# Order edges on VectorE kept in the gate-up groups of a hybrid encoder layer and dropped in its down and output projections

## The chip, the core and the metric

The kernel runs on one core of one Trainium2 chip. The metric is the device time of one execution, in microseconds. The core's engines that matter here are TensorE (PE in the profile), VectorE (DVE), ScalarE (ACT), GpSimd (POOL) and SyncE (SP), which issues nearly all transfers from memory.

## The reference

One encoder layer on 256 tokens of width 2048, all in float32: a gated feed-forward block, a mixer of two head groups, a second gated feed-forward block, each between two RMS norms.

```python
def swiglu(x, w_gate_up, w_down):
    gate, up = jnp.split(x @ w_gate_up, 2, axis=-1)          # 2048 -> 2 x 5632
    return (jax.nn.silu(gate) * up) @ w_down                 # 5632 -> 2048
...
    ff = swiglu(rms_norm(x, pre_norm_ffn1[layer]), w_ffn1_gate_up[layer], w_ffn1_down[layer])
    x = x + 0.5 * rms_norm(ff, post_norm_ffn1[layer])
    h = rms_norm(x, pre_norm_mix[layer])
    q_h, i_h, f_fwd, f_bwd, g_h, q_a, k_a, v_a = jnp.split(h @ w_mix_in[layer], split_at, axis=-1)
    y_h = hgrn2_mixer(...)          # gated linear recurrence, both directions, 8 heads
    y_a = window_attention(...)     # 8 heads, +-128 tokens
    mixed = jnp.concatenate([y_h, y_a], axis=-1) @ w_mix_out[layer]
    x = x + rms_norm(mixed, post_norm_mix[layer])
    ff = swiglu(rms_norm(x, pre_norm_ffn2[layer]), w_ffn2_gate_up[layer], w_ffn2_down[layer])
    x = x + 0.5 * rms_norm(ff, post_norm_ffn2[layer])
```

## The kernel before, in words

**Split operands.** Every float32 weight tile is written as a sum of two parts of a shorter format: a high part `h`, which ScalarE makes with a copy (line 191), and a lower part `l = raw - h`, which VectorE makes with a subtraction (line 192). A product of two split operands is three matmuls (line 447, method `three`): high by high, high by lower, lower by high. `split_half` (lines 180 to 188) splits one half, 128x1024, of a raw weight tile of 128x2048. Raw tiles lie in a ring of three, with a fourth one from the first gate-up group on and in the output projection (`rooms` in the feed-forward blocks); the `h` and the `l` tiles lie in two pools of five buffers each. A raw tile is loaded in two transfers of 512 KB, one for each half, and a transfer starts when the last reader of the old contents of that half is done.

**Units.** A stage of weights is worked off in units of 256 input rows by 1024 output columns. A plain unit (`plain`) takes 8 products, that is 24 matmuls. A mixed unit (`seven`) uses seven products instead of eight, a Strassen form with sums of blocks on both sides, and takes 21 matmuls. Its right-hand side costs VectorE three additions over the raw tile, in place: first `four` (line 480, 128x1024, two block sums at once), then the block `b22` (line 483, 128x512), then `b21` (line 484, 128x512, "the last addition"). Line numbers:

| step of `seven` | engine and line | what it needs |
|---|---|---|
| first block: `h`/`l`, or `ha`/`la` in the down stages and the output projection | ACT 191, DVE 192 | first half of the raw tile |
| `lower`: parts of the second half | ACT 191, DVE 192 | second half of the raw tile |
| three additions | DVE 480, 483, 484 | 480: first block split; 483: `lower` split and 480; 484: 483 |
| `upper`: parts of the summed first half | ACT 191, DVE 192 | 480 |
| `third`: parts of the summed second half | ACT 191, DVE 192 | 484 |

TensorE takes the seven products in the order first block, `lower`, `lower`, `upper`, `upper`, `third`, `third`.

**Stages.** The gate-up stages (class `Gated`, flag `AHEAD = False`) have 11 groups of 8 units, three of them mixed (two in group 1). The down stages and the output projection (class `Pairs`, flag `AHEAD = True`) have two runs each, one for each half of the output columns: 22 units a run in a down stage, 11 of them mixed; 8 units a run in the output projection, 2 of them mixed. In these, where a mixed unit is followed by a plain one, the plain unit's raw tile is loaded early and its first half (below: `v0`) is split between `upper` and `third` of the mixed unit (`begin_next`, lines 532 to 537); its second half (`v1`) comes after `third`. The input projection of the mixer, between them, has no mixed units but uses the same `split_half`.

**What sets the order.** The order of instructions in an engine's queue is not that of the program. A planner goes through the program when it is built; whenever an engine is free by its reckoning, it appends the earliest instruction of the program that is ready by its reckoning, so that a later instruction that is ready passes an earlier one that isn't yet. On the chip each queue is then worked off strictly in that order. `tc.issue_after(ins)` adds order edges: what its block puts on the engine of `ins` is queued behind `ins`. There is no wait in it, only a place in the queue. Here `last["sums"]` holds the newest `b21` addition, a VectorE instruction, so lines 184 to 187 tie the subtraction of line 192, and not ScalarE's copy, behind the last addition of the mixed unit that is newest in the program:

```python
        with ExitStack() as queued:
            if "sums" in last:
                queued.enter_context(tc.issue_after(last["sums"].ins))
            split_act(h, l, part)
```

The subtraction of the first block (`la`) is not made by `split_half` and has no such edge; nor have the additions.

Of the kernel before, what the change touches and what calls it, by code (L numbers as in the profile page):

```python
# [17 lines left out]
ALU = mybir.AluOpType  # L18
# [19 lines left out]
def hymba_layer_kernel(  # L38
# [25 lines left out]
    nc = tc.nc  # L64
# [15 lines left out]
    def pa():  # L80
        return psum.tile([P, 512], F32, tag="pa", name=nm("pa"))

    def pb():
        return psum.tile([P, 512], F32, tag="pb", name=nm("pb"))
# [64 lines left out]
    def load(src, between=None):  # L149
        raw = new_raw()  # L150
        if len(src.shape) == 4:

            dst = raw.rearrange("p (a n b) -> p a n b", a=src.shape[1], n=src.shape[2])
            parts = [(dst[:, a], src[:, a]) for a in range(src.shape[1])]
        else:
            n = src.shape[1]
            dst = raw.rearrange("p (a b) -> p a b", a=n)
            parts = [(dst, src)]
            if n == 2:
                parts = [(dst[:, a], src[:, a]) for a in range(2)]  # L160
        for i, (to, of) in enumerate(parts):
            if i and between:
                between()
            nc.sync.dma_start(to, of)
        return raw
# [14 lines left out]
    def split_half(raw, i, hp=hip, lp=lop):  # L180
        part = raw[:, i * 1024 : (i + 1) * 1024]
        h = hp.tile([P, 1024], F32R, tag="h", name=nm("h"))
        l = lp.tile([P, 1024], F32R, tag="l", name=nm("l"))
# [4 lines that stand above are left out]
        return h, l  # L188

    def split_act(hi, lo, src):  # L190
        nc.scalar.copy(hi, src)  # L191
        nc.vector.tensor_tensor(lo, src, hi.bitcast(F32), ALU.subtract)  # L192
# [37 lines left out]
    last = {}  # L230
# [179 lines left out]
    class Blocks:  # L410
# [58 lines left out]
        def seven(self, u, aside=None):  # L469

            self.left_early(u)
            raw = load(self.source(u))
            if aside:
                aside()
            b11, b12, b21, b22 = (raw[:, i * 512 : (i + 1) * 512] for i in range(4))
            four = raw.rearrange("p (i c) -> p i c", i=4)
            h, l = self.one_block()
            split_act(h, l, b11)
            lower = split_half(raw, 1)
            nc.vector.tensor_tensor(  # L480
                four[:, 0:2], four[:, 0::3], four[:, 1:2].to_broadcast([P, 2, 512]), ALU.add
            )
            nc.vector.tensor_tensor(b22, b11, b22, ALU.add)  # L483
            last["sums"] = nc.vector.tensor_tensor(b21, b22, b21, ALU.add)  # L484
            upper = split_half(raw, 0)
            if aside:
                aside()
            third = split_half(raw, 1)
            if not self.p:
                self.p = [pa(), pa(), pb(), pb()]  # L490
            a, w = self.tiles[u], self.left_sums(u)

            def lhs(k, m):
                return [a[:, k, i, m * P : (m + 1) * P] for i in range(2)]

            def summed(j):
                return [w[:, j, i, :] for i in range(2)]

            def rhs(two, n):
                return [x[:, n * 512 : (n + 1) * 512] for x in two]  # L500

            for at, left, right in (
                (("p", 0), lhs(0, 0), (h, l)),
                (("c", 0, 0), lhs(1, 0), rhs(lower, 0)),
                (("c", 0, 1), summed(S4), rhs(lower, 1)),
                (("p", 1), summed(S1), rhs(upper, 0)),
                (("p", 3), summed(S3), rhs(upper, 1)),
                (("p", 2), summed(S2), rhs(third, 1)),
                (("c", 1, 0), lhs(1, 1), rhs(third, 0)),
            ):  # L510
                self.three(at, *left, *right)
# [1095 lines left out]
```

## Time and profile before

| | |
|---|---|
| median of three runs | 1856.46 us (1854.08 to 1858.31) |
| the profiled execution | 1852.33 us, with a span of 1850.5 us |
| granted TensorE clock, mean | 0.999 |
| TensorE busy | 1828.6 us (99%) |
| VectorE busy | 1647.2 us (89%) |
| ScalarE busy | 1109.1 us (60%) |

The span is the time from the first to the last instruction that was profiled. "Idle before" is the time that an engine stood idle just before an instruction, and the releaser is what ended it. On SyncE all instructions are those of a queue that issues transfers; its time is waiting.

### The profile page before, as it was taken

To read this page: it belongs to the slowest core of one execution; us is meant where nothing else is said; L and a number is where in the kernel's file an instruction comes from. 1 tells how busy PE (TensorE), PEld (TensorE's weight loads), DVE (VectorE), ACT (ScalarE), POOL (GpSimd) and SP (SyncE) were. 2 spreads that over 40 slices of the span, in tenths; PEclk is the share of its full clock that TensorE was granted. 3 is DMA by queue.
4 is the path that set the end of the run, shared out by engine and by line. 5 is a ranking of instruction groups with operands and counts; after the bars stand their busy time and mean duration, and the time that the engine had idled before them with its cause. 6 is when DMAs were issued, how large, how long until landed. Compare 5 with 4: busy or idle time off the path is not lost.

```text
span 1850.5 us, 23957 instructions
## 1 busy us (share of the span) xinstructions
PE 1828.6 (99%) x8604; PEld 1517.0 (82%) x8604; DVE 1647.2 (89%) x2076; ACT 1109.1 (60%) x1470; POOL 33.3 (2%) x61
## 2 busy tenths in 40 slices
PE   9999999999999999999999999999999999999997
PEld 7888888888878777888888888888888888878776
DVE  7999999999999998577787798899999999989997
ACT  6555566565555556577677566555655555555553
POOL 1000000000000000000000000000000000000000
PEclk9999999999999999999999999999999999999999
DMA  8666566666877675655554565666666656778774
GB/s 286 200 229 210 194 203 218 211 201 215 283 256 266 228 248 197 217 177 174 168 181 153 187 218 184 202 231 214 208 221 222 212 195 199 254 260 269 244 254 169
DMA packets 192056, 400.45 MB, mean 216 GB/s; under 512 B 11976, under 2 KB 59168, under 8 KB 191168
## 3 DMA queue, kind: packets, MB, share of 16 engines
q1 hardware_dynamic: 188416, 387.24, 63.5%
q0 software_dynamic: 3520, 11.67, 1.6%
q8 instruction: 67, 1.10, 0.2%
q14 instruction: 53, 0.43, 0.1%
HBM read 383.12 MB, written 15.75 MB: 216 GB/s over the span
## 4 chain that ended last, share of the span: by engine, by line
PE 49%; issue 29%; DVE 12%; DMA 6%; ACT 3%; POOL 0%; SPq 0%; DVEq 0%; ACTq 0%; POOLq 0%
PE pa L447 16%; PE pb L447 15%; PE pa L322 8%; DVE l L192 7%; PE pa L327 4%; ACT h L191 2%; DMA raw<-in_w_ffn_down_dram 1%; DMA rooms<-in_w_ffn_down_dram 1%; DVE raw L480 1%; DMA raw<-in_w_ffn_gate_up_dram 1%; PE pa L377 1%; PE pa L376 1%; PE pa L375 1%; DVE raw L483 1%; DMA raw<-in_w_mix_out_dram 1%
## 5 line engine op out<-in xcount | busy, mean ns | idle before, releaser
L191 ACT CAST h<-raw 128x1024 fp32r<-128x1024 f32 (+1 forms) x691 | 682.4, 1014 | 425.0 <-DVE raw L484 118.9
L192 DVE TENSOR_TENSOR l<-raw,h 128x1024 fp32r<-128x1024 f32 (+1 forms) x691 | 795.2, 1174 | 77.9 <-ACT h L191 37.4
L447 PE MATMUL pa<-h,xt 128*128 128x512 f32 x1176 | 405.7, 391 | 0.0
L447 PE MATMUL pb<-h,xt 128*128 128x512 f32 x1060 | 368.9, 390 | 0.0
L447 PEld LDWEIGHTS pa<-h,xt 128*128 128x128 f32 x1176 | 220.8, 188 | 44.8
L447 PEld LDWEIGHTS pb<-h,xt 128*128 128x128 f32 x1060 | 198.9, 188 | 41.7 <-DVE xt L247 0.5
L447 PE MATMUL pa<-l,xt 128*128 128x512 f32 x588 | 229.5, 390 | 0.5 <-DVE l L192 0.5
L447 PE MATMUL pb<-l,xt 128*128 128x512 f32 x530 | 206.4, 389 | 0.0
L191 ACT CAST h<-rooms 128x1024 fp32r<-128x1024 f32 x138 | 142.1, 1050 | 90.1 <-DVE rooms L484 43.4
L192 DVE TENSOR_TENSOR l<-rooms,h 128x1024 fp32r<-128x1024 f32 x138 | 166.8, 1221 | 26.8 <-ACT h L191 26.3
L322 PE MATMUL pa<-xt,h 128*128 128x512 f32 x672 | 164.7, 394 | 0.0
L447 PE MATMUL pb<-h,ht 128*128 128x512 f32 x440 | 155.8, 390 | 2.0 <-DVE pb L528 2.0
L447 PE MATMUL pa<-h,ht 128*128 128x512 f32 x440 | 155.4, 391 | 0.0
L322 PEld LDWEIGHTS pa<-xt,h 128*128 128x128 f32 x672 | 123.0, 188 | 23.6
L447 PEld LDWEIGHTS pa<-l,xt 128*128 128x128 f32 x588 | 110.5, 188 | 24.2 <-DVE l L192 2.3
L447 PEld LDWEIGHTS pb<-l,xt 128*128 128x128 f32 x530 | 99.5, 188 | 20.6
L480 DVE TENSOR_TENSOR raw<-raw 128x1024 f32<-128x1024 f32 x92 | 112.2, 1220 | 1.7 <-DMA raw<-in_w_ffn_down_dram 0.7
L447 PEld LDWEIGHTS pb<-h,ht 128*128 128x128 f32 x440 | 82.6, 188 | 20.1 <-DVE pb L528 2.8
L447 PEld LDWEIGHTS pa<-h,ht 128*128 128x128 f32 x440 | 82.6, 188 | 18.3 <-issue 0.7
L327 PE MATMUL pa<-xt,l 128*128 128x256 f32 x672 | 91.8, 286 | 0.0
L327 PEld LDWEIGHTS pa<-xt,l 128*128 128x128 f32 x672 | 87.1, 191 | 3.2
L447 PE MATMUL pa<-l,ht 128*128 128x512 f32 x220 | 86.0, 391 | 0.4 <-DVE l L192 0.4
(280 smaller groups left out, 2478.6 us busy)
## 6 DMA issues: line engine op xcount, KB each, us to landing
raw<-in_w_ffn_gate_up_dram SPq DMA_DIRECT2D x270, 512.0 KB, 5.0
raw<-in_w_ffn_down_dram SPq DMA_DIRECT2D x132, 512.0 KB, 5.4
raw<-in_w_mix_in_dram SPq DMA_DIRECT2D x52, 1024.0 KB, 5.0
rooms<-in_w_ffn_gate_up_dram SPq DMA_DIRECT2D x80, 512.0 KB, 4.9
rooms<-in_w_ffn_down_dram SPq DMA_DIRECT2D x44, 512.0 KB, 5.1
sp<-ss SPq DMA_DIRECT2D x44, 512.0 KB, 7.0
raw<-in_w_mix_out_dram SPq DMA_DIRECT2D x32, 512.0 KB, 5.2
ss<-rooms POOLq DMA_DIRECT2D x22, 512.0 KB, 3.3
```

Source lines behind the costliest of these rows:

```text
L191: nc.scalar.copy(hi, src)
L192: nc.vector.tensor_tensor(lo, src, hi.bitcast(F32), ALU.subtract)
L322: nc.tensor.matmul(slot[f], weights(hs, kk, f), xcol(xt, k), start=(k == 0), stop=(k == KT - 1))
L327: nc.tensor.matmul(slot[f][:, 0:T], weights(ls, kk, f), xcol(xt, kh * 8 + kk, 0), start=False, stop=False,)
L375: nc.tensor.matmul(dst, xh, h[:, o : o + n], start=(k == 0), stop=False)
L376: nc.tensor.matmul(dst, xh, l[:, o : o + n], start=False, stop=False)
L377: nc.tensor.matmul(dst, xl, h[:, o : o + n], start=False, stop=(k == KT - 1))
L447: nc.tensor.matmul(self.bank(at), lhs, rhs, start=(n == 1), stop=n in (ends, self.of[at]), skip_group_check=n > ends,)
L480: nc.vector.tensor_tensor(four[:, 0:2], four[:, 0::3], four[:, 1:2].to_broadcast([P, 2, 512]), ALU.add)
L483: nc.vector.tensor_tensor(b22, b11, b22, ALU.add)
```

## The change

The last addition is still made in every mixed unit, but it is noted in `last["sums"]` in the gate-up stages alone. In the down stages and in the output projection `split_half` sees the last addition of the gate-up stage of the first feed-forward block (or, in the second block's down stage, of the second one), which is long past there. So the subtractions of `upper`, `third`, `v0`, `v1`, `lower` and of the plain units lose their order edge in these stages. No instruction is added, taken away or given another operand.

```diff
@@ -481,7 +481,9 @@
                 four[:, 0:2], four[:, 0::3], four[:, 1:2].to_broadcast([P, 2, 512]), ALU.add
             )
             nc.vector.tensor_tensor(b22, b11, b22, ALU.add)
-            last["sums"] = nc.vector.tensor_tensor(b21, b22, b21, ALU.add)
+            sums = nc.vector.tensor_tensor(b21, b22, b21, ALU.add)
+            if not self.AHEAD:
+                last["sums"] = sums
             upper = split_half(raw, 0)
             if aside:
                 aside()
```

## The prediction

> **What bounds the kernel now.** I read the page's first lines, then busy time by stage, then who waited for whom in the stages that the diff touches, then single rows of one pair of units.
>
> ```profile
> span 1850.5 us, 23957 instructions
> PE 1828.6 (99%) x8604; PEld 1517.0 (82%) x8604; DVE 1647.2 (89%) x2076; ACT 1109.1 (60%) x1470; POOL 33.3 (2%) x61
> ```
>
> TensorE is busy for 1828.6 of 1850.5 us, so all that could be had by taking away waits is 21.9 us. Where they lie, by stage (gate-up 1, its last group, the two runs of down 1, output projection, the two runs of down 2, tail):
>
> ```profile
> core 0: us, PE busy (x) PEld busy (x) DVE busy (x) ACT busy (x) POOL busy (x), PEclk, DMA share, GB/s
> 75.00:475.00 400.00, 400.00 (x1802) 331.34 (x1801) 380.79 (x438) 235.47 (x272) 4.27 (x8) 1.00 0.65 213
> 480.00:505.00 25.00, 25.00 (x116) 20.80 (x115) 23.42 (x33) 16.51 (x21) 1.07 (x2) 1.00 0.89 315
> 505.00:590.00 85.00, 83.70 (x366) 67.92 (x365) 77.64 (x80) 47.71 (x53) 0.00 (x0) 1.00 0.77 256
> 590.00:700.00 110.00, 106.99 (x459) 84.93 (x458) 104.40 (x112) 62.39 (x73) 0.00 (x0) 1.00 0.73 249
> 1050.00:1135.00 85.00, 84.35 (x373) 68.69 (x372) 75.41 (x92) 49.45 (x67) 0.56 (x1) 1.00 0.65 218
> 1630.00:1715.00 85.00, 83.33 (x364) 67.67 (x363) 78.98 (x81) 48.83 (x54) 0.00 (x0) 1.00 0.78 259
> 1715.00:1826.00 111.00, 108.90 (x471) 87.35 (x469) 106.82 (x115) 63.01 (x74) 0.00 (x0) 1.00 0.73 252
> 1826.00:1850.50 24.50, 15.06 (x65) 12.12 (x65) 10.81 (x22) 3.48 (x9) 2.38 (x3) 0.90 0.26 88
> ```
>
> The gate-up stage has no idle TensorE at all. The tail (9.4 us) is out of reach. The two down stages lose 1.30 + 3.01 and 1.67 + 2.10 us, 8.1 together, and the output projection 0.65. In the down stages VectorE is busy 91% to 96%: it paces TensorE there. What TensorE and VectorE wait for in down 1 (505 to 700) and in down 2 (1630 to 1826):
>
> ```profile
> PE pb L447 <- DVE l L192: 3.3, 6, 0.6
> PE pa L447 <- DVE l L192: 1.0, 4, 0.4
> DVE la L192 <- ACT ha L191: 6.5, 5, 1.9
> DVE l L192 <- ACT h L191: 2.7, 7, 0.8
> DVE rooms L480 <- DMA rooms<-in_w_ffn_down_dram: 1.7, 1, 1.7
> ...
> PE pb L447 <- DVE l L192: 2.9, 6, 0.6
> PE pa L447 <- DVE l L192: 0.6, 1, 0.6
> DVE la L192 <- ACT ha L191: 4.4, 4, 1.7
> DVE l L192 <- ACT h L191: 2.5, 6, 1.2
> ```
>
> TensorE waits for lower parts only, 4.3 and 3.5 us. Every pb row is one product: the first that uses `third`. VectorE itself idles before `la`, for ScalarE's `ha`. The rows of one pair of units say why (VectorE, then SyncE, ScalarE and TensorE; start, duration, the idle time before in brackets):
>
> ```profile
> 510.80 1.23 DVE L192 TENSOR_TENSOR l<-rooms,h 128x1024 fp32r<-128x1024 f32 x1 [0.26 <-ACT h L191]
> 512.06 0.69 DVE L483 TENSOR_TENSOR rooms<-rooms 128x512 f32<-128x512 f32 x1
> 512.67 1.22 DVE L480 TENSOR_TENSOR raw<-raw 128x1024 f32<-128x1024 f32 x1
> 513.80 0.69 DVE L484 TENSOR_TENSOR rooms<-rooms 128x512 f32<-128x512 f32 x1
> 514.40 1.22 DVE L192 TENSOR_TENSOR l<-rooms,h 128x1024 fp32r<-128x1024 f32 x1
> 515.54 1.22 DVE L192 TENSOR_TENSOR l<-raw,h 128x1024 fp32r<-128x1024 f32 x1
> 516.67 1.22 DVE L192 TENSOR_TENSOR l<-rooms,h 128x1024 fp32r<-128x1024 f32 x1
> 517.81 1.22 DVE L192 TENSOR_TENSOR l<-raw,h 128x1024 fp32r<-128x1024 f32 x1
> 520.97 0.69 DVE L192 TENSOR_TENSOR la<-rooms,ha 128x512 fp32r<-128x512 f32 x1 [1.94 <-ACT ha L191]
> 523.18 0.69 DVE L483 TENSOR_TENSOR raw<-raw 128x512 f32<-128x512 f32 x1
> 523.80 1.22 DVE L480 TENSOR_TENSOR rooms<-rooms 128x1024 f32<-128x1024 f32 x1
> 524.93 0.68 DVE L484 TENSOR_TENSOR raw<-raw 128x512 f32<-128x512 f32 x1
> ...
> 515.65 0.33 SPq L164 DMA_DIRECT2D rooms<-in_w_ffn_down_dram  x1
> ...
> 520.32 0.62 ACT L191 CAST ha<-rooms 128x512 fp32r<-128x512 f32 x1 [3.74 <-DMA rooms<-in_w_ffn_down_dram]
> 525.70 2.00 ACT L191 CAST h<-raw 128x1024 fp32r<-128x1024 f32 x2 [1.91 <-DVE raw L484]
> ...
> 527.85 0.61 PE L447 MATMUL pb<-h,sp 128*128 128x512 f32 x2
> 529.08 0.50 PE L447 MATMUL pb<-l,sp 128*128 128x512 f32 x1 [0.61 <-DVE l L192]
> ```
>
> VectorE's order is `lower` (510.80), line 483, the next unit's line 480, the last addition (513.80), `upper` (514.40), `v0`, `third` (516.67), `v1`. When `upper` ends at 515.62 the first half of `rooms` is free; SyncE issues its reload at 515.65, ScalarE gets the data at 520.32, and VectorE has meanwhile run dry for 1.94 us. So the reload, from the end of `upper` to the next `la`, is a loop that is some microseconds too long, and the edge sets when `upper` runs.
>
> **The change, part by part.** It adds and removes no instruction, no transfer and no semaphore wait; it frees places in VectorE's queue in 44 mixed units of the down stages and 4 of the output projection. TensorE's queue order is kept. SyncE's loads are moved with the halves that they refill; none is added. POOL has nothing in the down stages (x0 above).
>
> Which place is taken? Twice above, line 480 of the next unit, which has no edge, was put between lines 483 and 484: each addition needs the one before it, and the planner fills the gap with what is ready. Without the edge, `upper` and `v0` are candidates for these gaps, between `lower` and line 483 and between 483 and 484, and, being earlier in the program, they go before the next unit's line 480. I expect `lower`, `upper`, 483, `v0`, 484, `third`, or the same with `upper` one gap later.
>
> (a) Earlier `upper`. A 1024-wide subtraction takes 1.14 us from start to start (514.40 to 515.54), an addition 0.6. `upper` right behind `lower` would start at 510.80 + 1.26 = 512.06 instead of 514.40, 2.3 us earlier, or 1.7 one gap later (512.67); in a unit with nothing in the gap 1.2 or 0.6. The reload starts as much earlier. That covers the 1.94 us before `la` and the shorter waits of down 1 and 2. VectorE's idle time in these groups of waits is 6.5 + 2.7 + 1.7 and 4.4 + 2.5 us; TensorE can gain no more than what it loses at lower parts, 4.3 + 3.5 = 7.8 us by the rows. A matmul follows the last in 0.23 us, so the one at 529.08 came (529.08 - 528.08) - 0.23 = 0.77 late where the row says 0.61; with 0.16 more for each of 17 waits the upper bound is 10.5 us. The lower bound is nothing: the stalls at `third` stay if (b) eats the time. I take six tenths of 10.5, nearer to the upper bound because in the pair above the whole of the 1.94 is covered, though waits at the start of a run, where no earlier `upper` exists, are not: -6.3.
>
> (b) Later `third`. ScalarE's copy for `third` needs the last addition: it starts at 525.70, 0.09 after that addition's end at 525.61, and takes 1.05. Today `upper` and `v0` (2 x 1.14) run over this time. If both have gone ahead, `third` starts at 484's start + 0.68 + 0.09 + 1.05 + 0.1 = + 1.9, with 484 itself 2.28 later. Against today's 0.6 + 2.28 = 2.9 behind 484, that is 1.3 later at worst, and 0.2 where today the next unit's line 480 already sits in the gap (it is pushed behind 484 and covers the wait). TensorE is released late by that much once in a run, not in every unit: afterwards it follows VectorE later by the same amount, and VectorE's own work is unchanged, as long as something is ready to fill those 1.3 us (the next `la`, line 480, `v1`). Four runs give 0.8 to 5.2; I take 0.4 a run, nearer the lower end, since the unit whose `third` binds tends to have line 480 in the gap, as in both units above: +1.6.
>
> (c) A part that floats ahead may have to wait on the chip for its `h`, at the head of VectorE's queue, and holds the additions, `third` and the later loads behind it. The rows for such waits reach 0.8 and 1.2 us. For `upper` directly behind `lower` the copy is done (1.05 on ScalarE against 1.14 on VectorE), so I take 0.1 for a few units, +0.4; the end of the range is 44 x 0.1 = 4.4.
>
> (d) Output projection: four mixed units and 0.65 us of idle TensorE in all, so between -0.65 and 4 x 1.3 = +5.2. Zero, because its plain units outnumber the mixed ones three to one and cover them.
>
> (e) Gate-up and input projection: no edge that binds there is dropped; nothing.
>
> ```profile
> L483 DVE TENSOR_TENSOR raw<-raw 128x512 f32<-128x512 f32 x14 | 9.7, 690 | 0.4
> L484 DVE TENSOR_TENSOR raw<-raw 128x512 f32<-128x512 f32 x14 | 9.7, 690 | 0.3
> ```
>
> (f) The filled gaps themselves: the additions idle 0.4 + 0.3 us in a down stage (and less on `rooms`), so filling these gaps saves VectorE under 1 us a stage. I take nothing. [...]
>
> Sum: -6.3 + 1.6 + 0.4 = -4.3 us. The profiled execution, 1852.33 us (1.8 around the span of 1850.5), would become 1848.0; the median of the runs, 1856.46, becomes 1852.2.
>
> **The rivals.** A measurement of this kernel tells about 0.2%, 3.7 us, from no change; between the cases that is the border.
>
> *A, the forecast:* 1852, its own range 1846 to 1852.7, the lower end being 1856.46 - 10.5.
>
> *B, no difference.* Either the planner finds the freed parts not ready before the last addition, and the order stays (many units above and below have nothing between the additions though line 480 or `la` of the next is near), or (a) and (b) cancel, or the loads don't land earlier for being issued earlier. Against the last: down stages move 249 to 259 GB/s, and the window from 480 to 505 moved 315, so there is room. The Trainium skill, "DMA: Bandwidth & Descriptors", section "Specifications", puts the limit of one core's share of memory at about 358 GB/s; by that too the loads are not at a ceiling. Time 1853 to 1860.
>
> *C, slower: `third` without cover.* If VectorE has nothing ready in the 1.3 us before `third`, it stands idle, and then the price is paid in each unit whose `third` binds, not once a run. The 12 pb waits count these: 12 x 1.3 = 15.6, less the 2 or 3 that (a) returns: +13, 1869; with a share of the units 1861. It decides where the idle time added exceeds what VectorE now has free, 7.4 of 85 us in the first run. For it speaks that ScalarE's copies already idle 18.8 us of down 1 for line 484 on `raw` alone:
>
> ```profile
> L191 ACT CAST h<-raw 128x1024 fp32r<-128x1024 f32 x71 | 72.3, 1049 | 30.9 <-DVE raw L484 18.8 <-DVE raw L480 6.7 <-PE pb L447 2.5
> ```
>
> Against it speaks that the next `la` and line 480 have found places in this stretch.
>
> **How the numbers follow.** A 0.42, B 0.33, C 0.25. Predicted time 1852, A's. The range takes in A's lower end, 1846, B, and the larger part of C, up to 1866, and leaves out below 2 in 10. Faster by over 0.2% is A, 0.42; within it B, 0.33; slower C, 0.25.
>
> **What would show it.** Right: in the down stages line 192 stands between lines 483 and 484 or before 483; idle time before `la` falls from 6.5 to under 4 us in down 1; TensorE's waits for line 192 fall from 4.3 and 3.5 to about 2 each. Wrong: the same order (B); or larger idle time of VectorE before line 192 for ScalarE's `h`, and the pb waits grow beyond 0.6 us each (C).

## The result, and the profile after

The changed kernel took 1841.58 us (median of six runs) beside 1854.11 us for the kernel before: ratio 0.9932, 95% interval 0.9921 to 0.9942, a gain of 12.5 us. Timed twice more, beside the experiments, it gave 0.9950 (0.9936 to 0.9964) and 0.9945 (0.9931 to 0.9958), 8.6 and 9.6 us between the medians. The forecast was 4.3 us: the direction held, the size was missed by a factor of two to three, and the time lies below the range.

Single executions of the kernel before spread from 1847.5 to 1858.3 us, those of the changed one from 1840.8 to 1846.2. The profile used here (1845.24 us) is one of the long ones, so its difference to the profile before, 7.1 us, is smaller than that of the medians. Line numbers up to 484 are the same in both kernels; later ones are moved by two. The page's first lines, and the down stages by run, in the columns shown before:

```profile
span 1843.5 us, 23937 instructions
PE 1825.4 (99%) x8604; PEld 1519.5 (82%) x8604; DVE 1641.9 (89%) x2076; ACT 1106.1 (60%) x1470; POOL 33.2 (2%) x61
...
505.00:590.00 85.00, 84.81 (x374) 69.70 (x374) 77.72 (x82) 47.09 (x53) 0.00 (x0) 1.00 0.78 265
590.00:700.00 110.00, 107.53 (x467) 86.67 (x466) 105.21 (x116) 64.08 (x75) 0.00 (x0) 1.00 0.74 251
1630.00:1715.00 85.00, 82.77 (x363) 67.58 (x362) 76.31 (x81) 44.62 (x50) 0.00 (x0) 1.00 0.76 259
1715.00:1826.00 111.00, 109.39 (x479) 89.00 (x478) 104.55 (x114) 62.48 (x73) 0.00 (x0) 1.00 0.68 236
```

TensorE does more matmuls in the same windows of down 1: 374 instead of 366 and 467 instead of 459. (In down 2, which starts some 5 us earlier, the windows hold other parts of the work.) Who waited, in down 1 (505 to 700) and in down 2 (1630 to 1826):

```profile
PE pb L447 <- DVE l L192: 1.6, 3, 1.2
PE pa L447 <- DVE pa L526: 0.8, 1, 0.8
...
DVE l L192 <- ACT h L191: 7.9, 9, 1.2
DVE rooms L480 <- DMA rooms<-in_w_ffn_down_dram: 1.7, 1, 1.7
DVE la L192 <- ACT ha L191: 1.7, 2, 1.5
...
PE pb L447 <- DVE l L192: 2.1, 3, 1.2
PE pa L447 <- DVE pa L526: 1.3, 1, 1.3
...
DVE l L192 <- ACT h L191: 8.2, 8, 1.7
DVE la L192 <- ACT ha L191: 2.8, 2, 2.0
DVE rooms L480 <- DMA rooms<-in_w_ffn_down_dram: 0.8, 1, 0.8
```

TensorE's waits for lower parts fell from 4.3 to 1.6 us and from 3.5 to 2.1. VectorE's idle time did not fall: 11.3 us in these groups of down 1, against 6.5 + 2.7 + 1.7 = 10.9 before. It moved, from before `la` to before `l`. The same pair of units as in the prediction (VectorE; then SyncE and ScalarE):

```profile
509.01 2.35 DVE L192 TENSOR_TENSOR l<-rooms,h 128x1024 fp32r<-128x1024 f32 x2
511.28 0.68 DVE L483 TENSOR_TENSOR rooms<-rooms 128x512 f32<-128x512 f32 x1
511.88 1.22 DVE L192 TENSOR_TENSOR l<-raw,h 128x1024 fp32r<-128x1024 f32 x1
513.02 0.68 DVE L484 TENSOR_TENSOR rooms<-rooms 128x512 f32<-128x512 f32 x1
513.62 1.22 DVE L480 TENSOR_TENSOR raw<-raw 128x1024 f32<-128x1024 f32 x1
514.88 1.23 DVE L192 TENSOR_TENSOR l<-rooms,h 128x1024 fp32r<-128x1024 f32 x1
516.02 1.22 DVE L192 TENSOR_TENSOR l<-raw,h 128x1024 fp32r<-128x1024 f32 x1
517.46 0.69 DVE L192 TENSOR_TENSOR la<-rooms,ha 128x512 fp32r<-128x512 f32 x1 [0.22 <-ACT ha L191]
521.36 1.23 DVE L480 TENSOR_TENSOR rooms<-rooms 128x1024 f32<-128x1024 f32 x1 [1.73 <-DMA rooms<-in_w_ffn_down_dram]
522.50 0.69 DVE L483 TENSOR_TENSOR raw<-raw 128x512 f32<-128x512 f32 x1
...
512.03 0.33 SPq L164 DMA_DIRECT2D rooms<-in_w_ffn_down_dram  x1
...
516.80 0.62 ACT L191 CAST ha<-rooms 128x512 fp32r<-128x512 f32 x1 [1.01 <-DMA rooms<-in_w_ffn_down_dram]
```

The order is the one that was forecast: `lower` and `upper` (509.01, two of them), 483, `v0` (511.88), 484, line 480 of the next mixed unit, `third` (514.88), `v1`. The reload of `rooms` starts at 512.03 instead of 515.65, `la` runs at 517.46 instead of 520.97, and 1.94 us of idle time became 0.22. The reload starts right behind line 483, which ends at 511.96: that line reads the first half too, and with `upper` ahead of it it is the half's last reader. The row at 521.36 shows the remaining trouble. Now the unit in `raw` is the present one, and line 480 of the next mixed unit, in `rooms`, stands in the queue ahead of its line 483; the load isn't there, and VectorE waits 1.73 us with 483, 484 and lower parts of the present unit behind it.

Where the time went: the start of the n-th matmul of TensorE's queue, minus its start before, and how this difference changed over each part (us; below zero is time gained; parts by the times of the profile before). The prediction said that TensorE's order is kept; it is the same in both kernels but for 22 places at the ends of the down stages, and some 50 places differ in the last two columns. The last three columns are profiles of the experiments below.

| part | changed, first profile | changed, 1842.59 us | `d1_hold_next` | `b2_before_short` |
|---|---|---|---|---|
| down 1, first run (505 to 592) | -1.9 | -2.2 | -2.5 | -2.5 |
| end of that run, additions to the banks (592 to 596) | +1.2 | +1.6 | -0.2 | -0.2 |
| down 1, second run (596 to 700) | -3.5 | -4.3 | -5.8 | -6.0 |
| end of down 1 (700 to 720) | -1.0 | -1.1 | -0.5 | -1.5 |
| output projection (1050 to 1170) | +0.2 | +0.2 | +0.6 | +0.8 |
| down 2, first run (1630 to 1718) | -1.3 | -2.9 | -2.9 | -2.9 |
| end of that run (1718 to 1722) | +1.9 | +1.4 | 0.0 | 0.0 |
| down 2, second run (1722 to 1824.5) | -2.2 | -2.5 | -1.9 | -4.2 |
| end of down 2 (1824.5 to 1830) | -0.7 | -0.9 | -0.2 | -1.2 |

The end of a first run costs the changed kernel time. In both kernels VectorE waits there for the `la` of a unit ahead, with the additions to the banks behind it (first the row before, then the row after):

```profile
586.66 0.69 DVE L192 TENSOR_TENSOR la<-raw,ha 128x512 fp32r<-128x512 f32 x1 [1.35 <-ACT ha L191]
...
586.07 0.69 DVE L192 TENSOR_TENSOR la<-raw,ha 128x512 fp32r<-128x512 f32 x1 [1.49 <-ACT ha L191]
```

Before, TensorE came to this place 1.7 us later and did not have to wait for the additions.

### The profile page after: what moved, and what is told of

It is laid out like the page before. It is cut to its first block, busy times and chain, and to the rows that moved or that the text cites. A ratio compares the mean times of both kernels' runs of the same rounds, so it can differ in the third digit from the quotient of the medians.

```text
span 1843.5 us, 23937 instructions
## 1 busy us (share of the span) xinstructions
PE 1825.4 (99%) x8604; PEld 1519.5 (82%) x8604; DVE 1641.9 (89%) x2076; ACT 1106.1 (60%) x1470; POOL 33.2 (2%) x61
## 4 chain that ended last, share of the span: by engine, by line
PE 75%; DVE 14%; issue 4%; DMA 4%; ACT 3%; POOL 0%; SPq 0%; DVEq 0%; ACTq 0%; POOLq 0%
PE pa L447 29%; PE pb L447 27%; PE pa L322 8%; DVE l L192 8%; PE pa L327 4%; ACT h L191 2%; DMA raw<-in_w_mix_out_dram 1%; DMA raw<-in_w_ffn_down_dram 1%; DVE raw L480 1%; PE pa L377 1%; PE pa L376 1%; PE pa L375 1%; DVE raw L483 1%; DVE raw L484 1%; DVE la L192 1%
```

## The experiments

Kernels of one batch share their runs of the kernel before: 17 runs, median 1851.82 us, for the first batch; 9 runs, 1852.21, for the second; 11 runs, 1852.68, for the third.

**Which part of the change: `upper` alone, the down stages alone, and the reload.** `a0_after` and `f0_after` are the changed kernel.

> The changed kernel once more, for a second profile and as the partner of the runs beside it. Three theories of its gain of about 12.5 us. R (reload): `upper` earlier frees the first half of a raw tile earlier, the reload starts earlier and VectorE no longer runs dry before `la`. D (direct): TensorE simply gets lower parts earlier, the time of the reload does not matter. E (elsewhere): a part comes from the output projection or from the ends of the runs. All three: 0.9932 of before again, 11 to 14 us. If the profiled execution falls near 1841.5 us, its difference to the first profile (1845.2 us) shows where single executions of the same queue differ.

Measured: 0.9950 (0.9936 to 0.9964), median 1843.24 us.

`a1_upper_free`, on the kernel before (shortened):

```diff
-    def split_half(raw, i, hp=hip, lp=lop):
+    def split_half(raw, i, hp=hip, lp=lop, free=False):
...
-            if "sums" in last:
+            if "sums" in last and not free:
...
-            upper = split_half(raw, 0)
+            upper = split_half(raw, 0, free=self.AHEAD)
```

> The kernel before, with the order edge taken from the lower part of `upper` alone in the down stages and the output projection; `lower`, `v0`, `third`, `v1` and the plain units keep it. R: the reload of the first half is all that counts, so most of the gain is there, -9 to -13 us. D: `v0` and the plain parts are still late, so about half, -4 to -7 us. E: says nothing of this.

Measured: 0.9979 (0.9968 to 0.9990), median 1848.27 us, -3.6 us, below both expectations and nearest to D's; single runs from 1844.6 to 1852.2. With `upper` alone freed, less than half of the gain is there, though the reload of `rooms` in the example starts at 512.01, as early as in the changed kernel. A version with `v0` alone freed was not run.

`a3_down_only`, on the changed kernel (shortened):

```diff
-            if not self.AHEAD:
+            if not getattr(self, "stored", False):
                 last["sums"] = sums
```

> The changed kernel, with the edges kept in the output projection, so that only the two down stages are free of them. R and D: within 1 us of the changed kernel, since TensorE idles for 0.65 us there in all. E: 2 us or more of the gain is lost.

Measured: 0.9947 (0.9934 to 0.9959), median 1842.95 us, 0.3 us from the changed kernel beside it. The output projection has no part in the gain that shows; what the ends of the runs give and take stands in the table above.

`a4_late_reload`, on the changed kernel, and `b0_before_late`, the same edit on the kernel before (shortened):

```diff
+        if len(src.shape) == 3 and src.shape[1] == 2:
+            second = nc.sync.dma_start(*parts[1])
+            with tc.issue_after(second.ins):
+                nc.sync.dma_start(*parts[0])
+            return raw
         for i, (to, of) in enumerate(parts):
```

> The changed kernel, but in the down stages and the output projection the transfer of a raw tile's first half is queued on SyncE behind that of its second half, so that it can't start before `third` (or `v1`) is done; VectorE's order is nearly that of the changed kernel. R: the gain is lost, between -3 us and +8 us against before. D: the gain stays, -9 us or better.

Measured: 0.9938 (0.9924 to 0.9951), median 1840.82 us, if anything better than the changed kernel. The reload of `rooms` was indeed late (second half, then first half):

```profile
517.91 0.33 SPq L162 DMA_DIRECT2D rooms<-in_w_ffn_down_dram  x1
518.29 0.42 SPq L164 DMA_DIRECT2D rooms<-in_w_ffn_down_dram  x1
```

That is 2.6 us later than before the change (515.65) and 6.3 later than after it. So an earlier reload is not needed for the gain. What this kernel also changes is the plan: the next unit's `la` and line 480 stand at 514.81 and 515.53 in it, behind `v0`, and at 508.41 and 513.62 in the changed kernel. The theory R fell here, and the next one is about that.

> The kernel before, edges and all, with the transfer of a raw tile's first half queued on SyncE behind that of its second half in the down stages and the output projection. The changed kernel kept its whole gain with such late reloads (about -11 us against before), so theory R (earlier reloads) is in doubt. New theory U (urgency): what costs is that the first block and the block sum of the next mixed unit, which have no edge, pass `v0` and `third` of the present one, which have; a late reload makes the planner place them later. R: later reloads make it slower, +2 to +10 us. U: the next unit's work is planned later, so a gain, -3 to -9 us. Nothing, within 2 us, if only the places of `upper` and `v0` themselves count.

Measured: 0.9936 (0.9924 to 0.9949), median 1839.38 us. With every old edge in place the kernel gains 12.8 us. Its `la` and line 480 of the next unit stand at 513.11 and 515.20, behind `upper` (510.43) and `v0`, and before at 509.85 and 512.67, ahead of both. The reload of `rooms` starts at 515.70, as before (515.65), though `upper` ran 4.0 us earlier. By TensorE's progress (the matmuls begun when the reload of a first half of `rooms` starts, at 0.2275 us each; median of 22 reloads) the reloads come 1.6 us later than before here and 1.9 later in `a4_late_reload`; in the changed kernel they come 1.3 and 1.8 us earlier, by two profiles. R is refuted in the form "the reload must be earlier", and so is the idea that the edges cost by themselves.

**The next unit's work, held back directly.** `d1_hold_next`, on the kernel before (shortened; line 480's addition is at 486 in it, and `last["low"]` is the newest subtraction of line 192):

```diff
-            split_act(h, l, b11)
+            with ExitStack() as behind:
+                if self.AHEAD and "third" in last:
+                    behind.enter_context(tc.issue_after(last["third"].ins))
+                split_act(h, l, b11)
...     # the same around the addition of line 480
             third = split_half(raw, 1)
+            last["third"] = last["low"]     # its subtraction
```

> The kernel before, with all its edges, and in the down stages and the output projection the first block's subtraction and the addition of line 480 of a mixed unit also queued behind the lower part of `third` of the mixed unit before, so that VectorE takes unit after unit. U: -5 to -12 us, as much as the change. R: reloads start no earlier, `upper` stays behind the last addition: within 3 us of before. If the passing work was a welcome filling of VectorE's gaps: +5 us or more.

Measured: 0.9935 (0.9922 to 0.9947), median 1839.95 us, -12.3 us, as much as U said or a little more. VectorE's rows for the second unit of the pair, `lower`, then `upper`, `v0` and `third`, then the next unit's `la`:

```profile
518.90 1.23 DVE L192 TENSOR_TENSOR l<-raw,h 128x1024 fp32r<-128x1024 f32 x1 [1.48 <-ACT h L191]
520.16 0.69 DVE L489 TENSOR_TENSOR raw<-raw 128x512 f32<-128x512 f32 x1
520.89 0.69 DVE L490 TENSOR_TENSOR raw<-raw 128x512 f32<-128x512 f32 x1
521.50 3.49 DVE L192 TENSOR_TENSOR l<-raw,h 128x1024 fp32r<-128x1024 f32 x3
524.91 0.68 DVE L192 TENSOR_TENSOR la<-rooms,ha 128x512 fp32r<-128x512 f32 x1
```

Before, `la` and line 480 of that next unit stood at 520.97 and 523.80, ahead of these parts, and the `third` here, the third of the three that start at 521.50, began at 527.80; now it begins at about 523.8. This run alone does not decide between U and R: with `upper` at 510.94 the reload of `rooms` starts at 512.19, as early as in the changed kernel, while R's expectation took reloads to start no earlier. The runs with later reloads decide it. What is held back is not urgent: in the profile before, `la` runs 11.6 us (median of 48) before TensorE's first matmul with it. ScalarE's queue had the same fault before: `ha` waited 3.74 us for its load (the row at 520.32 in the prediction), and copies of the present unit, whose loads had landed by 513.20, came right behind it, and then `lower` on VectorE:

```profile
520.84 2.95 ACT L191 CAST h<-raw 128x1024 fp32r<-128x1024 f32 x3
...
521.92 1.23 DVE L192 TENSOR_TENSOR l<-raw,h 128x1024 fp32r<-128x1024 f32 x1 [0.26 <-ACT h L191]
```

An instruction at the head of a queue that waits for a load holds up ready work behind it. The Trainium skill, "Perfetto Trace Analysis", section "Tensor Engine Instruction (MATMUL, LD_WEIGHTS)", says that ScalarE and VectorE work strictly first in, first out; the rows here agree, with those copies behind the 3.74 us of waiting.

**The loads themselves, made short.** `b1_after_short` and `b2_before_short`: in the down stages a quarter of the columns of each weight tile is loaded, the rest keeps old numbers (shortened).

```diff
                 parts = [(dst[:, a], src[:, a]) for a in range(2)]
+                if short["on"]:        # set in the down stages
+                    parts = [(to[:, 0:256], of[:, 0:256]) for to, of in parts]
```

> The kernel before, with only a quarter of the columns of each weight tile loaded in the down stages (the rest of the tile keeps what it held, so its down projections are of other numbers); the transfers are of 128 KB instead of 512 KB and land sooner, VectorE's order is nearly that of before. R: the waits before `la` go, -6 to -10 us. U: the order still lets the next unit pass, so most of the loss stays, 0 to -4 us.

> The changed kernel with the same short loads in the down stages (three quarters of each tile not loaded). R: nearly nothing more to gain, it falls together with the kernel before with short loads, both about -10 us against before. U: it keeps its distance to the kernel before with short loads, 6 us or more, and gains 0 to -4 us on the changed kernel, -9 to -15 us against before.

Measured: on the kernel before 0.9904 (0.9889 to 0.9920), median 1834.21 us; on the changed one 0.9910 (0.9896 to 0.9923), median 1835.21. Transfers into `raw` landed in 2.4 us instead of 5.4. They fall together at -17 to -18 us. That they do is what R said of the pair, and U's expectation of a kept distance missed; both had the gain too small (R 6 to 10 us, U up to 4, for the kernel before). TensorE's two down stages (505 to 700 and 1630 to 1818) in the kernel before with short loads, and, below the dots, with its full loads:

```profile
505.00:700.00 195.00, 195.00 (x862) 161.24 (x861) 189.83 (x201) 117.95 (x132) 0.00 (x0) 1.00 0.40 126
1630.00:1818.00 188.00, 188.00 (x831) 155.47 (x830) 177.64 (x191) 108.90 (x122) 0.00 (x0) 1.00 0.34 107
...
505.00:700.00 195.00, 190.69 (x823) 152.85 (x822) 182.03 (x191) 110.10 (x126) 0.00 (x0) 1.00 0.75 252
1630.00:1818.00 188.00, 184.30 (x802) 149.21 (x801) 177.81 (x186) 107.83 (x123) 0.00 (x0) 1.00 0.75 253
```

With loads that land in time the edges cost nothing, and TensorE has no idle time. The next unit's work still goes ahead in the queue, as these rows of VectorE in the kernel before with short loads show (480 and 483 are at 484 and 487 in it): `la` and line 480 of the unit in `rooms` stand ahead of line 483 of the present unit, in `raw`.

```profile
516.66 0.68 DVE L196 TENSOR_TENSOR la<-rooms,ha 128x512 fp32r<-128x512 f32 x1
517.38 1.23 DVE L484 TENSOR_TENSOR rooms<-rooms 128x1024 f32<-128x1024 f32 x1
518.52 1.22 DVE L196 TENSOR_TENSOR l<-raw,h 128x1024 fp32r<-128x1024 f32 x1
519.77 0.69 DVE L487 TENSOR_TENSOR raw<-raw 128x512 f32<-128x512 f32 x1
```

So passing alone costs nothing either. The two halves, R's and U's, make one theory, H: the cost before is the wait for late loads at the head of the queues, with urgent parts behind; it goes when the loads are there, or when what needs them stands further back.

**Together.** `d2_after_hold_next` is the changed kernel with the edge of `d1_hold_next`; `e1_hold_late` the kernel before with that edge and the late reload; `c1_no_queue` has no edge behind the last addition anywhere (the two lines of the changed kernel that set `last["sums"]` left out).

> The changed kernel a third time, as the partner of the three beside it: 8 to 13 us below before. Theory H (head of queue), formed from the earlier runs: before, the first block of the next mixed unit stands in the queues of ScalarE and VectorE ahead of parts of the present unit, its load lands later than planned, and the whole queue waits; short loads, later planning and the change each take this away in their own way.

> The changed kernel with the first block's subtraction and the addition of line 480 of a mixed unit queued behind the lower part of `third` of the mixed unit before. H: the change and this edge take away the same wait, so together they give no more than the edge alone: -10 to -15 us against before. If the change's own moves of `upper` and `v0` were worth something beside it, -16 us or more, towards the -18 of the short loads.

> The kernel before with that edge and with the late reload of the first halves, both, and the old edges kept. H: again the same wait, -10 to -16 us against before; if reload time matters once nothing passes, the late reload costs here, -3 to -9 us.

> No order edges behind the last addition anywhere, in the gate-up stages neither. TensorE has no idle time there with the edges. If the gate-up groups have slack enough (VectorE is busy 381 of 400 us there, so little), it equals the changed kernel within 2 us; if `third` without cover then binds, it is 4 to 30 us slower than the changed kernel.

Measured: `f0_after` 0.9945 (0.9931 to 0.9958), 1843.06 us. `d2_after_hold_next` 0.9970 (0.9959 to 0.9981), 1848.16 us: only -4.5, a miss of the expectation. Its rows in down 1 (TensorE, then VectorE):

```profile
PE pb L447 <- DVE l L192: 2.1, 5, 0.6
PE pa L447 <- DVE l L192: 0.8, 2, 0.4
...
DVE l L192 <- ACT h L191: 5.9, 5, 1.2
```

Here `upper` and `v0` go ahead of the last addition, and nothing of the next unit may fill the time until `third`'s copy is done: VectorE idles 1.2 us at a time before it. That is rival C of the prediction, with its condition: TensorE's named waits for lower parts, counted from start to start, are 8.7 us, with 10.5 before. It isn't the whole: this kernel also loses 2.8 us in the output projection.

`e1_hold_late` 0.9908 (0.9894 to 0.9921), 1836.18 us: -16.5 us, the best version with all the work in it, 7 us under the changed kernel. The late reload did not cost (its reloads come 1.0 us later than before by the count above), and the two add up to more than H said.

`c1_no_queue` 0.9956 (0.9944 to 0.9969), 1845.21 us, 2.2 us more than `f0_after`, between the two expectations. In its one profile the two gate-up stages take 1.6 and 1.9 us longer than before, so the edges there are worth something: 2.2 us by the medians.

What was not separated: how much of the change's gain comes from the earlier reload and how much from `upper` and `v0` passing the next unit, since each edit made the planner lay all queues anew, and a new order can by itself be worth some us. Nor whether VectorE's queue or ScalarE's cost more.

## Why the prediction was wrong in size

**The new order and the earlier reload: right.** `upper` and `v0` went into the gaps and displaced the next unit's line 480, as said; the reload in the example came 3.6 us earlier, 2.3 were forecast. Idle time before `la` fell from 6.5 to 1.7 us in down 1 (under 4 was forecast).

**Term (a), the gain at stake: mis-sized, and the main failure.** I bounded it by TensorE's rows of waits for lower parts, 7.8 us, plus 0.16 us for each, 10.5, and took six tenths. Short loads show what waits for loads cost in all: 17 to 18 us. Start to start, TensorE's matmuls of the down stages were late by 10.0 and 8.3 us in the profile before (505 to 703 and 1630 to 1830, the sum of what exceeds 0.2275 us between neighbours). The same sum, by what the matmul waited for:

| us late, both down stages | before | changed, first profile | changed, 1842.88 us | changed, 1842.59 us |
|---|---|---|---|---|
| rows of waits for lower parts | 10.5 | 4.7 | 3.5 | 2.6 |
| ends of the stages (line 528, 530 in the changed kernel) | 2.3 | 0.7 | 0.4 | 0 |
| ends of the first runs (526 in the changed kernel) | 0 | 2.4 | 1.6 | 2.3 |
| small delays without a row | 5.5 | 3.4 | 3.5 | 3.0 |
| sum | 18.3 | 11.2 | 9.0 | 7.8 |

So the 10.5 were right for what they counted, and 7.8 us were left out. One part is small delays, each of which leaves TensorE less than 0.15 us idle. The other is the wait for line 528 at the ends of the stages (0.98 us at 702.5 and at 1826.9, the second of which I had put out of reach with the tail); before and after, in the first profile:

```profile
PE pb L447 <- DVE pb L528: 1.0, 1, 1.0
...
PE pb L447 <- DVE pb L530: 0.2, 1, 0.2
```

At the rows that were counted the change took away 5.8 to 7.9 us, with the prices of (b) and (c) in it, where -6.3 + 1.6 + 0.4 = -4.3 was forecast. What was not counted gave 3.8 to 4.9 more, and the ends of the first runs took 1.6 to 2.4 back. All in all that is 40 to 60% of 18.3 in these profiles, and 50 to 70% by the medians, 8.6 to 12.5 us: that my six tenths fit the larger sum is luck, since they came from the reload loop. The range's lower end, taken from the same bound, fell with it. The base was off too: 1856.46 us was the median of three runs, and six runs gave 1854.11, so 2.35 of the 10.6 us between the forecast time and the measured one are not a matter of the change.

**The reasoning under (a): half right.** I took the reload loop for the pace of VectorE. `a4_late_reload` and `b0_before_late` have later reloads and gain as much. What matters is what stands behind the instruction that waits for a load. I had named the displacement of the next unit's line 480 and counted it only as cover for `third`; by these runs holding it back gains by itself. That the reload starts as much earlier as `upper` was not so either: behind `upper` it waits for line 483.

**Term (b), later `third`, +1.6:** VectorE's idle time before lower parts rose from 2.7 to 7.9 us in down 1, in waits up to 1.2 us, so a sign of C is there. TensorE did not pay for it in each unit: in the first profile it waits 1.2 us for a lower part once in each down stage, at 622.92 and at 1745.83, 2.7 us together from start to start. VectorE is not idle there; `la` and line 480 of the next unit fill the time before `third` (621.64), as (b) said, and `third` is late all the same:

```profile
619.18 0.69 DVE L484 TENSOR_TENSOR rooms<-rooms 128x512 f32<-128x512 f32 x1
619.78 0.68 DVE L192 TENSOR_TENSOR la<-raw,ha 128x512 fp32r<-128x512 f32 x1
620.50 1.23 DVE L480 TENSOR_TENSOR raw<-raw 128x1024 f32<-128x1024 f32 x1
621.64 1.22 DVE L192 TENSOR_TENSOR l<-rooms,h 128x1024 fp32r<-128x1024 f32 x1
```

C did not decide here, and does in `d2_after_hold_next`.

**Term (c), +0.4,** can't be told apart in (b)'s rows. **(d), zero:** right, `a3_down_only`. **(f), nothing for filled gaps:** it was sized from rows of idle time, and these say too little. From start to start an addition that needs the one before it comes 0.73 us behind (520.16 to 520.89 in `d1_hold_next`), a subtraction that doesn't need it 0.60 (511.28 to 511.88 in the changed kernel). No run separates what the filled gaps gave; VectorE's idle time did not fall.

## What to carry to other kernels

Here the idle time of the pacing engine said less than what stood behind it: look for an instruction at the head of a queue that waits for a load while ready work that the next engine needs lies behind. Hold back early work on the next unit before making its load faster; an order edge that keeps urgent work late while later units' work has no edge is half a rule. To bound what waits are worth, sum the start-to-start excess of the engine that sets the end, or make the loads short for one run: rows of named waits were a factor of two too low here.

## What the runs showed of the hardware

In down 1 (505 to 700) a transfer of 512 KB into `raw` landed in 5.2 us, with the memory at 252 GB/s, and one of 128 KB in 2.4, at 126 GB/s (medians, in the profiles of the kernel before with full and with short loads). And the kernel whose TensorE waited for no load had the steadier time: four runs between 1833.9 and 1834.4 us, against 1847.5 to 1858.3 in all runs of the kernel before. That late loads make the spread is not shown.
